# Layer 1's attention with unnormalised probabilities, divided once per eight units

## The chip, the core and the metric

The kernel runs on one NeuronCore of a Trainium2 chip. The metric is the time of one execution in microseconds of the device; the median of three runs of the kernel before is 2408.08 us (2406.07 to 2408.76). The core has five engines with queues of their own, which run in order and wait for each other by semaphores: TensorE (PE; its weight loads are listed as PEld), VectorE (DVE), ScalarE (ACT), GpSimd (POOL) and SyncE (SP), which here issues the transfers. Matmul results land in PSUM, everything else lives in SBUF.

## The reference

A two-layer encoder over 1024 positions of width 1024. Layer 1 mixes with windowed attention (16 query heads in 4 groups that share keys and values, window +-128, a learned sink logit per head), layer 2 with dilated attention; each layer ends in a SwiGLU network. What the change touches is the attention of layer 1, cut to its core:

```
s = einsum('nbqhgd,nbkhd->nbhgqk', qb, kw) * (dh ** -0.5) + bias      # 128 queries x 384 keys
m = max(s.max(axis=-1), sink)
p = exp(s - m)
l = p.sum(axis=-1) + exp(sink - m)
o = einsum('nbhgqk,nbkhd->nbqhgd', p, vw) / l
```

All of it is float32. The kernel keeps that accuracy on PE by splitting each operand into a rounded high part and a low remainder, and by multiplying the parts.

## The kernel before

Layer 1's attention is `layer_a`. Its work comes in 32 units: 2 halves of the sequence (t), 4 key heads (hd), 4 blocks of 128 queries each (b). A unit has two parts, written as generators that yield between steps. `first` calls `probs`: for each of the 4 query heads g, two matmuls write the scores 128 queries x 384 keys (256 at the sequence's ends) into a PSUM tile ps_s (two buffers); DVE adds the bias, takes the negated maximum and writes the tile p (line 509); ACT takes the exponential and the sum l (line 519). Then the kernel before forms the denominator: n plus the sink (line 516), its exponential (517), the sum (522), the reciprocal (523), and it scales the four tiles p, three on DVE (526) and one on ACT (528).

`second` calls `weigh` two units later: for each block of 128 keys PE transposes the four tiles p into ps_t (548, two buffers), ACT copies the high part to pp (550), DVE subtracts for the low part (551), and two matmuls weigh the values into ps_o (542). The values hold high and low parts side by side, so ps_o has the two halves of a sum in its two halves of partitions; ACT copies one (563), DVE adds the other (564) into os. ACT and POOL split os into the two parts of oT (813, 814), which the output projection reads.

Between these steps `weave` places fill work by the table FILL_A: the projections of the second half's queries, the output projection of the first half (`out_0`, whose result is added to x by line 370 and squared for the norm of the next network), and the first matmuls of that network. A scheduler orders the instructions of each engine from this text with costs of its own, and gives tiles their buffers: p has a ring of 11, the bias tiles one of 6, and the general tiles t2 (os, the rows of x and their squares) one of 4.

After the last unit the queue is emptied: the norm of the first half (rms on PE and POOL, `modulate` on DVE and ACT), the first matmuls of the network (`up_early`), the last weighings, and the output projection of the second half. Its weights pass through ACT (179) and POOL (180), which split them as well.

Of the kernel before, what the change touches and what calls it, by code (L numbers as in the profile page):

```python
# [74 lines left out]
class Trunk:  # L75
# [419 lines left out]
    def probs(self, psp, att, qs, kh, kl, lo, hi, bias, sink, n, l, width, bufs, zero=None):  # L495


        nc = self.nc
        per, np = bufs
        tiles = [att.tile([P, per, width], F, name="p", tag="p", bufs=np) for _ in range(4 // per)]  # L500
        pt = [p[:, g] for p in tiles for g in range(per)]
        for p in tiles if zero else ():
            nc.gpsimd.memset(p[:, :, zero], 0.0)
        for g in range(4):
            ps = psp.tile([P, HT], F, name="ps_s", tag="s", bufs=2)
            nc.tensor.matmul(ps[:, lo:hi], lhsT=qs[g], rhs=kh, start=True, stop=False)  # L506
            mm = nc.tensor.matmul(ps[:, lo:hi], lhsT=qs[g], rhs=kl, start=False, stop=True)
            self.marks.append(mm.ins)
            nc.vector.tensor_tensor_reduce(pt[g][:, lo:hi], ps[:, lo:hi], bias[g][:, lo:hi], -1.0,  # L509
                                           -NEG if sink is None else sink[1][:, g:g + 1],  # L510
                                           op0=ALU.add, op1=ALU.min, accum_out=n[:, g:g + 1])
            yield
        if sink is not None:
            st = att.tile([P, 2, 4], F, name="st", tag="st", bufs=6)
            e, r = st[:, 0], st[:, 1]
            nc.vector.tensor_tensor(e, sink[0], n, op=ALU.add)
            nc.scalar.activation(e, e, AF.Exp)
        for g in range(4):
            nc.scalar.activation(pt[g][:, lo:hi], pt[g][:, lo:hi], AF.Exp, bias=n[:, g:g + 1], scale=-1.0, accum_out=l[:, g:g + 1])
        if sink is None:  # L520
            return pt
        nc.vector.tensor_tensor(l, l, e, op=ALU.add)
        nc.vector.reciprocal(r, l)
        for g in range(4):
            if g < 3:
                nc.vector.tensor_scalar(pt[g][:, lo:hi], pt[g][:, lo:hi], r[:, g:g + 1], None, op0=ALU.mult)  # L526
            else:
                nc.scalar.activation(pt[g][:, lo:hi], pt[g][:, lo:hi], AF.Copy, scale=r[:, g:g + 1])
        return pt

    def weigh(self, psp, att, pt, chunks, out, low, par):
# [191 lines left out]
    def layer_a(self, h, x_src):  # L723
# [65 lines left out]
        self.norm_bank = self.bank  # L789
        wp, wk = (es.enter_context(sb(n)) for n in ("probs_a", "work_a"))  # L790
        self.raw = deque([(self.main, 1)])
        dist = wp.tile([P, 384], F, name="dist")
        nc.sync.dma_start(dist, a["dist"][:, 0:384])

        def first(hd, b, bias):
# [1 line left out]
            lo, hi = (0 if b > 0 else P), (384 if b < 7 else 256)  # L797
            k0 = (b - 1) * P
            c = slice((b % 4) * P, (b % 4) * P + P)
            ml = wp.tile([P, 2, 4], F, name="ml", tag="ml", bufs=6)  # L800
            return self.probs(psp, wp, [q[(p, g, par, t)][:, c] for g in range(4)], kh[hd][:, k0 + lo:k0 + hi], kl[hd][:, k0 + lo:k0 + hi],
                              lo, hi, bias, [self.sink[:, s, 4 * hd:4 * hd + 4] for s in range(2)], ml[:, 0], ml[:, 1], 384, (1, 11))

        def second(hd, b, pt, oT):
            p, par = hd // 2, hd % 2
            own, other = head_rows(par)
            cs = [c for c in range(3) if 0 <= b - 1 + c <= 7]
            os = wk.tile([P, HT], F, name="os", tag="t2", bufs=self.t2)
            osv = os.rearrange("p (g q) -> p g q", q=P)
            yield from self.weigh(psp, wk, pt, [(c * P, vt[:, b - 1 + c, hd], P) for c in cs], osv[own], osv[other], par)  # L810
            osv = osv[own]
            c = slice((b % 4) * P, (b % 4) * P + P)
            nc.scalar.activation(oT[p][0][own, :, c], osv, AF.Copy)
            nc.gpsimd.tensor_tensor(oT[p][1][own, :, c], osv, f32(oT[p][0][own, :, c]), op=ALU.subtract)

        def out_proj(ps, d, oT):
            return self.project_steps(ps, self.weight("a_w_out", d), [(oT[k // 4][0][:, k % 4], oT[k // 4][1][:, k % 4]) for k in range(KT)])
# [10 lines left out]
            if d == KT - 1:  # L828
                spill["h"] = self.norm_half(spill["x"], spill["ssq"], layer, 1, wk)

        oTs = []
        self.fill_start([q_tile(p, g, 1) for p in range(2) for g in range(4)] + [out_0(d) for d in range(KT)] + [self.up_early(layer, spill)], FILL_A, LOOK_A, 64)
        units = [(t, hd, b) for t in range(2) for hd in range(4) for b in range(4 * t, 4 * t + 4)]
        pend = deque()
        for i, (t, hd, b) in enumerate(units):
# [4 lines left out]
            if i in (16, 24):  # L840
                self.fill_until(32 * (i // 8 - 1))
            if b % 4 == 0:
                bias = self.bias_tiles(wp, dist, SLOPE_A[4 * hd:4 * hd + 4], 6, nc.vector if i < BIAS_DVE else None)
            pt = self.weave(i, first(hd, b, bias), second(*pend.popleft()) if len(pend) > 1 else None)
            pend.append((hd, b, pt, oTs[t]))
        while self.fill:
            self.fill_step()
        while pend:
            run(second(*pend.popleft()))
        es.close()  # L850
        self.kqv.close()

# [449 lines left out]
def _arrays(np, i):  # L1302
# [8 lines left out]
    def per_part(v):  # L1311
# [3 lines left out]
    o["x"] = c(i["x"][0].T).reshape(KT, P, T)  # L1315
    o["vec"] = c(np.concatenate([per_part(i["norm_mix"]), per_part(i["norm_ffn"]), per_part(i["final_norm"]),
                                 per_part(i["c"]), per_part(i["ada_b"])], axis=1))
    o["sink"] = c(i["a_sink"])
    o["cst"], o["dist"] = _constants(np)
    o["ada_w"] = c(i["ada_w"])  # L1320
# [42 lines left out]
```

## Time and profile before

| | us |
|---|---|
| median of three runs | 2408.08 |
| the profiled execution | 2409.9 |
| its span | 2408.1 |
| PE busy | 2264.6 (94%) |
| DVE busy | 1286.4 (53%) |
| ACT busy | 870.2 (36%) |
| POOL busy | 740.7 (31%) |

Times of rows are microseconds from the span's start. A row of a group gives the line of the kernel, the engine and operation, what it writes and reads, the shapes and the count; behind the first bar the busy time and the mean duration of one in ns, behind the second the idle time of that engine just before such an instruction, and who ended it. PE overlaps matmuls, so a duration can be longer than the distance to the next one.

### The profile page before, as it was taken

The numbers are of one execution on the slowest core, as the hardware profiler recorded it, in microseconds if no ns is written. First come the engines' busy times: TensorE is split into PE (matmuls) and PEld (weight loads), VectorE is DVE, ScalarE is ACT, GpSimd is POOL, SyncE is SP. The second block draws the span as 40 slices with busy tenths as digits, with TensorE's granted clock in tenths as the row PEclk, the third lists the DMA queues.
The fourth block names the chain that finished last, engine by engine and source line by source line (L and its number), as shares of the span: only waits on it lengthen the run. The fifth ranks groups of instructions, "written<-read, shape, count | busy, mean of one in ns | idle before, by whom it ended". The sixth has DMA issues, their size and how long they took to land.

```text
span 2408.1 us, 28177 instructions
## 1 busy us (share of the span) xinstructions
PE 2264.6 (94%) x10572; PEld 1874.8 (78%) x10572; DVE 1286.4 (53%) x2263; ACT 870.2 (36%) x1721; POOL 740.7 (31%) x467
## 2 busy tenths in 40 slices
PE   8699898988999999999989999787999999999997
PEld 7587676766788888888879878665788888888886
DVE  6869999688533333333362577785633332222325
ACT  2549887332111111111252788673411111111111
POOL 2525453453122122222233344344531212221210
PEclk9899999999999999999999999898999999999999
DMA  7431124666411111111234765736321111111101
GB/s 282 154 139 36 40 84 132 215 218 207 158 59 39 50 44 53 44 53 44 79 123 156 197 185 179 214 88 195 102 71 53 48 49 53 53 52 46 53 18 70
DMA packets 131225, 248.85 MB, mean 103 GB/s; under 512 B 39312, under 2 KB 66576, under 8 KB 130064
## 3 DMA queue, kind: packets, MB, share of 16 engines
q1 hardware_dynamic: 131088, 247.05, 32.1%
q8 instruction: 83, 1.36, 0.2%
q14 instruction: 54, 0.44, 0.1%
HBM read 214.20 MB, written 30.70 MB: 102 GB/s over the span
## 4 chain that ended last, share of the span: by engine, by line
PE 70%; DVE 15%; DMA 6%; issue 2%; ACT 2%; SPq 1%; POOL 0%; DVEq 0%; ACTq 0%; POOLq 0%
PE ps_d L300 22%; PE ps_d L302 22%; PE ps_d L301 22%; DMA ada_w<-in_ada_w 3%; DVE ada_acc L152 2%; DVE p L509 2%; DVE pp L551 2%; DVE p L526 1%; PE ps_o L542 1%; PE ps_t L548 1%; DVE os L564 1%; DVE ht L272 1%; DMA ml_all<-sd 1%; DVE h L278 1%; DMA al<-ad 1%
## 5 line engine op out<-in xcount | busy, mean ns | idle before, releaser
L300 PE MATMUL ps_d<-h,w 128*128 128x512 f32 x1968 | 778.1, 397 | 29.3 <-ACT w L179 14.2
L301 PE MATMUL ps_d<-h,w 128*128 128x512 f32 x1968 | 777.0, 395 | 10.9 <-DVE h L278 9.3
L302 PE MATMUL ps_d<-h,w 128*128 128x512 f32 x1968 | 773.7, 394 | 2.6 <-POOL w L180 2.6
L180 POOL TENSOR_TENSOR w<-raw,w 128x1024 fp32r<-128x1024 f32 (+1 forms) x178 | 431.7, 2427 | 786.6 <-ACT w L179 774.7
L300 PEld LDWEIGHTS ps_d<-h,w 128*128 128x128 f32 x1968 | 373.9, 190 | 101.5 <-ACT w L179 15.7
L301 PEld LDWEIGHTS ps_d<-h,w 128*128 128x128 f32 x1968 | 375.3, 191 | 83.4 <-DVE h L278 11.7
L302 PEld LDWEIGHTS ps_d<-h,w 128*128 128x128 f32 x1968 | 373.9, 190 | 82.1 <-POOL w L180 3.8
L417 DVE TENSOR_TENSOR u<-silu,ps_d 128x512 f32<-128x512 f32 x88 | 60.4, 686 | 605.9 <-PE ps_d L302 589.7
L370 DVE SCALAR_TENSOR_TENSOR x<-ps_d,mod,x 128x512 f32<-128x512 f32 x368 | 270.4, 748 | 152.0 <-PE ps_d L302 149.5
L179 ACT ACTIVATE w<-raw 128x1024 fp32r<-128x1024 f32 (+1 forms) x178 | 185.7, 1047 | 368.4 <-PE ps_d L302 295.0
L300 PE MATMUL ps_d<-act,wo 128*128 128x512 f32 x704 | 276.1, 392 | 10.0 <-DVE x L370 6.9
L302 PE MATMUL ps_d<-act,wo 128*128 128x512 f32 x704 | 275.0, 391 | 0.0
L301 PE MATMUL ps_d<-act,wo 128*128 128x512 f32 x704 | 274.9, 391 | 0.0
L180 POOL TENSOR_TENSOR wo<-raw,wo 128x1024 fp32r<-128x1024 f32 x44 | 106.4, 2417 | 432.7 <-ACT wo L179 425.2
L179 ACT ACTIVATE wo<-raw 128x1024 fp32r<-128x1024 f32 x44 | 46.7, 1061 | 382.5 <-PE ps_d L302 340.3
L300 PEld LDWEIGHTS ps_d<-act,wo 128*128 128x128 f32 x704 | 132.6, 188 | 39.5 <-DVE x L370 8.3
L302 PEld LDWEIGHTS ps_d<-act,wo 128*128 128x128 f32 x704 | 132.7, 188 | 27.7
L301 PEld LDWEIGHTS ps_d<-act,wo 128*128 128x128 f32 x704 | 132.7, 188 | 27.1
L419 DVE TENSOR_TENSOR act<-u,act 128x512 fp32r<-128x512 f32 x88 | 125.1, 1421 | 47.5 <-ACT act L418 47.4
L152 DVE SCALAR_TENSOR_TENSOR ada_acc<-ada_w,cond,ada_acc 128x1024 f32<-128x1024 f32 x70 | 125.9, 1799 | 43.2 <-DMA ada_w<-in_ada_w 42.6
L418 ACT ACTIVATE act<-u 128x512 fp32r<-128x512 f32 x88 | 55.0, 625 | 217.1 <-DVE u L417 217.1
L506 PE MATMUL ps_s<-kh,q 128*128 128x384 f32 (+3 forms) x320 | 103.6, 328 | 21.4 <-DVE stat L509 11.5
(174 smaller groups left out, 2660.1 us busy)
## 6 DMA issues: line engine op xcount, KB each, us to landing
raw<-in_ffn_w_in SPq DMA_DIRECT2D x102, 512.0 KB
ada_w<-in_ada_w SPq DMA_DIRECT2D x80, 512.0 KB
raw<-in_ffn_w_out SPq DMA_DIRECT2D x44, 512.0 KB
raw<-in_b_w_q SPq DMA_DIRECT2D x24, 512.0 KB
qd<-qo SPq DMA_DIRECT2D x48, 256.0 KB
h<-in_ada_w SPq DMA_DIRECT2D x8, 1024.0 KB
raw<-in_a_w_out SPq DMA_DIRECT2D x16, 512.0 KB
q<-qd SPq DMA_DIRECT2D x16, 512.0 KB
```

Source lines behind the costliest of these rows:

```text
L152: nc.vector.scalar_tensor_tensor(acc, w, s, acc, op0=ALU.mult, op1=ALU.add)
L179: self.nc.scalar.activation(w[:, 0], raw, AF.Copy)
L180: self.nc.gpsimd.tensor_tensor(w[:, 1], raw, f32(w[:, 0]), op=ALU.subtract)
L300: mm(ps, lhsT=w[0], rhs=x[0], start=first, stop=False)
L301: mm(ps, lhsT=w[0], rhs=x[1], start=False, stop=False)
L302: mm(ps, lhsT=w[1], rhs=x[0], start=False, stop=last)
L370: self.nc.vector.scalar_tensor_tensor(x, ps, self.mod[:, layer, c * 8 + d:c * 8 + d + 1], x, op0=ALU.mult, op1=ALU.add)
L417: nc.vector.tensor_tensor(u, s, up, op=ALU.mult)
L418: nc.scalar.activation(act[:, 0, halves(t)], u, AF.Copy)
L419: nc.vector.tensor_tensor(act[:, 1, halves(t)], u, f32(act[:, 0, halves(t)]), op=ALU.subtract)
L506: nc.tensor.matmul(ps[:, lo:hi], lhsT=qs[g], rhs=kh, start=True, stop=False)
L509: nc.vector.tensor_tensor_reduce(pt[g][:, lo:hi], ps[:, lo:hi], bias[g][:, lo:hi], -1.0, -NEG if sink is None else sink[1][:, g:g + 1], op ...
```

## The change

The probabilities of layer 1 are weighed as they come from the exponential. n and l of eight units (a pair of heads, one half of the sequence) are kept in a tile ml, the weighed sums of the eight units in a tile ou of 128 x 4 x 512 (one buffer). A new function `normalise` runs once for each such block, after unit 9, 17 and 25 and at the end: it forms the 32 denominators' reciprocals of each query in one go, splits them into high and low parts, transposes them (four 128 x 16 transposes), and multiplies the 16 rows with a matrix sel of zeros and ones, so that PE writes each reciprocal to the 64 partitions of its head. DVE multiplies ou with that, and ACT and POOL split the product. The ring of p becomes 9, that of the bias tiles 5.

```diff
@@ probs @@
             nc.vector.tensor_tensor_reduce(pt[g][:, lo:hi], ps[:, lo:hi], bias[g][:, lo:hi], -1.0,
-                                           -NEG if sink is None else sink[1][:, g:g + 1],
+                                           -NEG if sink is None else sink[:, g:g + 1],
                                            op0=ALU.add, op1=ALU.min, accum_out=n[:, g:g + 1])
             yield
-        if sink is not None:
-            st = att.tile([P, 2, 4], F, name="st", tag="st", bufs=6)
-            e, r = st[:, 0], st[:, 1]
-            nc.vector.tensor_tensor(e, sink[0], n, op=ALU.add)
-            nc.scalar.activation(e, e, AF.Exp)
         for g in range(4):
             nc.scalar.activation(pt[g][:, lo:hi], pt[g][:, lo:hi], AF.Exp, bias=n[:, g:g + 1], scale=-1.0, accum_out=l[:, g:g + 1])
-        if sink is None:
-            return pt
-        nc.vector.tensor_tensor(l, l, e, op=ALU.add)
-        nc.vector.reciprocal(r, l)
-        for g in range(4):
-            if g < 3:
-                nc.vector.tensor_scalar(pt[g][:, lo:hi], pt[g][:, lo:hi], r[:, g:g + 1], None, op0=ALU.mult)
-            else:
-                nc.scalar.activation(pt[g][:, lo:hi], pt[g][:, lo:hi], AF.Copy, scale=r[:, g:g + 1])
         return pt
@@ layer_a @@
+        sel = wp.tile([16, HT], R, name="sel")
+        raw = wk.tile([P, HT], F, name="sel_f", tag="t2", bufs=self.t2)[0:16]
+        nc.sync.dma_start(raw, a["sel"])
+        nc.scalar.activation(sel, raw, AF.Copy)
...
-            ml = wp.tile([P, 2, 4], F, name="ml", tag="ml", bufs=6)
+            if hd % 2 == 0 and b % 4 == 0:
+                mls[p, t] = wp.tile([P, 2, 2, 4, 4], F, name="ml", tag="ml", bufs=2)
+            ml = mls[p, t][:, :, par, b % 4]
...
-                              lo, hi, bias, [self.sink[:, s, 4 * hd:4 * hd + 4] for s in range(2)], ml[:, 0], ml[:, 1], 384, (1, 11))
+                              lo, hi, bias, self.sink[:, 1, 4 * hd:4 * hd + 4], ml[:, 0], ml[:, 1], 384, (1, 9))
...
-            os = wk.tile([P, HT], F, name="os", tag="t2", bufs=self.t2)
-            osv = os.rearrange("p (g q) -> p g q", q=P)
-            yield from self.weigh(psp, wk, pt, [(c * P, vt[:, b - 1 + c, hd], P) for c in cs], osv[own], osv[other], par)
-            osv = osv[own]
+            if par == 0 and b % 4 == 0:
+                outs[p, t] = wk.tile([P, 4, HT], F, name="ou", tag="ou", bufs=1)
+            low = wk.tile([P, HT], F, name="os", tag="t2", bufs=self.t2)
             c = slice((b % 4) * P, (b % 4) * P + P)
-            nc.scalar.activation(oT[p][0][own, :, c], osv, AF.Copy)
-            nc.gpsimd.tensor_tensor(oT[p][1][own, :, c], osv, f32(oT[p][0][own, :, c]), op=ALU.subtract)
+            yield from self.weigh(psp, wk, pt, [(c * P, vt[:, b - 1 + c, hd], P) for c in cs], outs[p, t][own, :, c],
+                                  low.rearrange("p (g q) -> p g q", q=P)[other], par)
+
+        def normalise(p, t, oT):
+
+            n, l = (mls[p, t][:, s] for s in range(2))
+            e = wp.tile([P, 2, 4, 4], F, name="e", tag="e", bufs=1)
+            sink = self.sink[:, 0, 8 * p:8 * p + 8].rearrange("p (h x g) -> p h x g", h=2, x=1).broadcast_to([P, 2, 4, 4])
+            nc.vector.tensor_tensor(e, sink, n, op=ALU.add)
+            nc.scalar.activation(e, e, AF.Exp)
+            nc.vector.tensor_tensor(l, l, e, op=ALU.add)
+            nc.vector.reciprocal(e, l)
+            fl = wp.tile([P, 4, 2, 8], R, name="fl", tag="fl", bufs=1)
+            ev = e.rearrange("p h b g -> p b h g")
+            hi, lo = (fl[:, :, s].rearrange("p b (h g) -> p b h g", h=2) for s in range(2))
+            nc.scalar.activation(hi, ev, AF.Copy)
+            nc.vector.tensor_tensor(lo, ev, f32(hi), op=ALU.subtract)
+            tp = psp.tile([P, HT], F, name="ps_t", tag="t", bufs=2)
+            for b in range(4):
+                nc.tensor.transpose(tp[0:16, b * P:(b + 1) * P], f32(fl[:, b]).rearrange("p s x -> p (s x)"), self.ident)
+            rows = wk.tile([P, HT], R, name="rows", tag="t2", bufs=self.t2)[0:16]
+            nc.scalar.activation(rows, tp[0:16], AF.Copy)
+            for g in range(4):
+                ps = psp.tile([P, HT], F, name="ps_r", tag="s", bufs=2)
+                nc.tensor.matmul(ps, lhsT=sel[:, g * P:(g + 1) * P], rhs=rows, start=True, stop=True)
+                o = wk.tile([P, HT], F, name="os", tag="t2", bufs=self.t2)
+                nc.vector.tensor_tensor(o, outs[p, t][:, g], ps, op=ALU.mult)
+                nc.scalar.activation(oT[p][0][:, g], o, AF.Copy)
+                nc.gpsimd.tensor_tensor(oT[p][1][:, g], o, f32(oT[p][0][:, g]), op=ALU.subtract)
...
-                bias = self.bias_tiles(wp, dist, SLOPE_A[4 * hd:4 * hd + 4], 6, nc.vector if i < BIAS_DVE else None)
+                bias = self.bias_tiles(wp, dist, SLOPE_A[4 * hd:4 * hd + 4], 5, nc.vector if i < BIAS_DVE else None)
             pt = self.weave(i, first(hd, b, bias), second(*pend.popleft()) if len(pend) > 1 else None)
-            pend.append((hd, b, pt, oTs[t]))
+            pend.append((hd, b, pt))
+            if i % 8 == 1 and i > 1:
+                normalise(i // 8 % 2 ^ 1, (i - 2) // 16, oTs[(i - 2) // 16])
...
             run(second(*pend.popleft()))
+        normalise(1, 1, oTs[1])
```

In the rows of the order that follow, the new kernel's lines are numbered anew: its 514 is the exponential (before 519), 528 the weighing (542), 534 the transpose (548), 537 the low part pp (551), 550 the sum of the two halves, now into ou (564), 828 the spread matmul into ps_r, 830 the product.

DVE near the end of the units, before, up to the last addition to x (line 370), where ISA is the score read:

```order
L526 TENSOR_SCALAR p<-p,st 128x384 x3
L509 ISA p,ml<-ps_s,bias,sink 128x256
L509 ISA ml 128x1
L509 ISA p,ml<-ps_s,bias,sink 128x256
L509 ISA ml 128x1
L551 TENSOR_TENSOR pp<-ps_t,pp 128x512
L564 TENSOR_TENSOR os<-ps_o,os 64x512
L370 SCALAR_TENSOR_TENSOR xst<-ps_d,mod,xst 128x512
```

The same place now, from the first score read of the last unit on:

```order
L509 ISA p,ml<-ps_s,bias,sink 128x256
L509 ISA ml 128x1
L550 TENSOR_TENSOR ou<-ps_o,os 64x4x128
L537 TENSOR_TENSOR pp<-ps_t,pp 128x512
L370 SCALAR_TENSOR_TENSOR xst<-ps_d,mod,xst 128x512
L509 ISA p,ml<-ps_s,bias,sink 128x256
L509 ISA ml 128x1
```

The three scalings are gone, and the addition stands ahead of the last unit's second score read.

PE among the scores of units 8 to 11 before: scores (506, 507), fill (300 to 302), weighing and transposes:

```order
L507 MATMUL ps_s<-kl_85,q 128x384
L300 MATMUL ps_d<-h,w 128x512
L301 MATMUL ps_d<-h,w 128x512
L302 MATMUL ps_d<-h,w 128x512
L548 MATMUL ps_t<-cst,p 128x128 x4
L542 MATMUL ps_o<-pp,vt 128x512 x3
L548 MATMUL ps_t<-cst,p 128x128 x4
L506 MATMUL ps_s<-kh_81,q 128x384
```

PE at the first block now, which stands among the scores of the same units:

```order
L302 MATMUL ps_d<-h,w 128x512
L528 MATMUL ps_o<-pp,vt 128x512 x2
L534 MATMUL ps_t<-cst,p 128x128 x4
L828 MATMUL ps_r<-rows,sel 128x512 x2
L534 MATMUL ps_t<-cst,p 128x128 x4
L528 MATMUL ps_o<-pp,vt 128x512 x2
L534 MATMUL ps_t<-cst,p 128x128 x4
L528 MATMUL ps_o<-pp,vt 128x512
L828 MATMUL ps_r<-rows,sel 128x512 x2
L528 MATMUL ps_o<-pp,vt 128x512 x2
L534 MATMUL ps_t<-cst,p 128x128 x4
L506 MATMUL ps_s<-kh_81,q 128x384
```

The spread matmuls come in two pairs, and no score or fill matmul stands from the first pair until the row after the second.

PE between the first matmuls of the network and the output projection, before:

```order
L301 MATMUL ps_d<-h,w 128x512
L302 MATMUL ps_d<-h,w 128x512
L542 MATMUL ps_o<-pp,vt 128x512 x4
L300 MATMUL ps_d<-h,w 128x512
L301 MATMUL ps_d<-h,w 128x512
```

And now:

```order
L302 MATMUL ps_d<-h,w 128x512
L528 MATMUL ps_o<-pp,vt 128x512 x4
L828 MATMUL ps_r<-rows,sel 128x512 x4
L300 MATMUL ps_d<-h,w 128x512
L301 MATMUL ps_d<-h,w 128x512
```

The four spread matmuls of the last block stand between the last weighing and the output projection.

## Rows read from the trace of the kernel before

**Rows 1.** The page's first line.

```profile
span 2408.1 us, 28177 instructions
```

**Rows 2.** Stretches: PE, PEld, DVE, ACT, POOL busy (instructions), PE clock, DMA, GB/s.

```profile
165.00:394.50 229.50, 212.94 (x1110) 172.79 (x1111) 221.35 (x564) 199.39 (x480) 104.64 (x71) 0.99 0.19 61
394.50:416.20 21.70, 14.21 (x71) 10.56 (x69) 18.58 (x41) 14.27 (x31) 6.30 (x15) 0.84 0.58 195
...
660.00:720.00 60.00, 60.00 (x267) 49.69 (x266) 23.03 (x26) 10.86 (x14) 14.93 (x7) 1.00 0.19 59
1332.00:1500.00 168.00, 164.17 (x926) 137.33 (x925) 115.84 (x380) 140.39 (x393) 68.70 (x58) 0.99 0.66 188
```

**Rows 3.** Groups on DVE, 165 to 394.5 us.

```profile
L551 DVE TENSOR_TENSOR pp<-ps_t,pp 128x512 fp32r<-128x512 f32 x79 | 54.0, 684 | 0.8 <-ACT pp L550 0.2
L526 DVE TENSOR_SCALAR p<-p,st 128x384 f32<-128x384 f32 x69 | 37.8, 603 | 0.4
...
L516 DVE TENSOR_TENSOR st<-sink,ml 128x4 f32<-128x4 f32 x30 | 12.9, 431 | 0.1
...
L522 DVE TENSOR_TENSOR ml<-ml,st 128x4 f32<-128x4 f32 x30 | 9.3, 310 | 0.1
L526 DVE TENSOR_SCALAR p<-p,st 128x256 f32<-128x256 f32 x21 | 7.6, 420 | 0.2
L523 DVE RECIPROCAL st<-ml 128x4 f32<-128x4 f32 x30 | 5.3, 176 | 0.7
```

**Rows 4.** Groups on PE, 165 to 394.5 us.

```profile
L542 PE MATMUL ps_o<-pp,vt 128*128 128x512 f32 x158 | 62.6, 430 | 9.4 <-DVE pp L551 8.9 <-ACT pp L550 0.3
...
L506 PE MATMUL ps_s<-kh,q 128*128 128x384 f32 x96 | 36.5, 380 | 3.4 <-DVE ml L509 3.1
...
L506 PE MATMUL ps_s<-kh,q 128*128 128x256 f32 x27 | 8.8, 328 | 3.0 <-DVE ml L509 3.0
```

**Rows 5.** Groups on ACT, then on POOL, 165 to 394.5 us.

```profile
L550 ACT ACTIVATE pp<-ps_t 128x512 fp32r<-128x512 f32 x80 | 46.7, 587 | 3.3 <-PE ps_t L548 2.5
...
L813 ACT ACTIVATE h<-os 64x512 fp32r<-64x512 f32 x28 | 17.6, 627 | 6.1 <-DVE os L564 5.6
...
L528 ACT ACTIVATE p<-p,st 128x384 f32<-128x384 f32 x23 | 13.9, 606 | 0.1
...
L814 POOL TENSOR_TENSOR h<-os,h 64x512 fp32r<-64x512 f32 x28 | 36.1, 1288 | 75.4 <-ACT h L813 71.2 <-DMA raw<-in_a_w_out 3.7
```

**Rows 6.** Timeline of DVE, then of POOL: start, us, instruction.

```profile
326.52 1.08 DVE L526 TENSOR_SCALAR p<-p,st 128x384 f32<-128x384 f32 x3
...
396.95 3.17 DVE L526 TENSOR_SCALAR p<-p,st 128x384 f32<-128x384 f32 x3
...
397.55 2.36 POOL L180 TENSOR_TENSOR w<-raw,w 128x1024 fp32r<-128x1024 f32 x1 [4.01 <-ACT w L179]
```

**Rows 7.** Timeline at the stage's end: PE, SP and DVE.

```profile
394.25 0.39 PE L302 MATMUL ps_d<-h,w 128*128 128x512 f32 x1
...
395.44 0.42 SPq L585 DMA_DIRECT2D xst<-in_x  x1
...
402.28 0.75 DVE L370 SCALAR_TENSOR_TENSOR xst<-ps_d,mod,xst 128x512 f32<-128x512 f32 x1
...
406.56 0.95 PE L222 MATMUL ps_d<-ones,ssq 128*128 128x1 f32 x8
...
411.58 1.16 PE L260 MATMUL ps_d<-cst,st 128*128 128x128 f32 x8 [0.93 <-POOL st L257]
...
416.22 0.57 PE L301 MATMUL ps_d<-h,w 128*128 128x512 f32 x1 [1.38 <-DVE h L278]
```

**Rows 8.** Timeline at the output projection of the second half.

```profile
428.97 1.09 PE L542 MATMUL ps_o<-pp,vt 128*128 128x512 f32 x4
...
430.82 0.68 DVE L564 TENSOR_TENSOR os<-ps_o,os 64x512 f32<-64x512 f32 x1 [0.89 <-ACT os L563]
...
431.56 0.50 PE L300 MATMUL ps_d<-h,w 128*128 128x512 f32 x1 [1.50 <-DVE os L564]
...
434.43 2.37 POOL L180 TENSOR_TENSOR w<-raw,w 128x1024 fp32r<-128x1024 f32 x1
```

More of the change, by code (lines that the diff above doesn't have):

```diff
@@ L804, in second @@
-        def second(hd, b, pt, oT):
-            p, par = hd // 2, hd % 2
+                              lo, hi, bias, self.sink[:, 1, 4 * hd:4 * hd + 4], ml[:, 0], ml[:, 1], 384, (1, 9))
+        def second(hd, b, pt):
+            p, par, t = hd // 2, hd % 2, b // 4
             own, other = head_rows(par)
             cs = [c for c in range(3) if 0 <= b - 1 + c <= 7]
-            os = wk.tile([P, HT], F, name="os", tag="t2", bufs=self.t2)
-            osv = os.rearrange("p (g q) -> p g q", q=P)
-            yield from self.weigh(psp, wk, pt, [(c * P, vt[:, b - 1 + c, hd], P) for c in cs], osv[own], osv[other], par)
-            osv = osv[own]
+            if par == 0 and b % 4 == 0:
+                outs[p, t] = wk.tile([P, 4, HT], F, name="ou", tag="ou", bufs=1)
+            low = wk.tile([P, HT], F, name="os", tag="t2", bufs=self.t2)
@@ L829, in out_0 @@
                 spill["h"] = self.norm_half(spill["x"], spill["ssq"], layer, 1, wk)
-        oTs = []
+        oTs, mls, outs = [], {}, {}
         self.fill_start([q_tile(p, g, 1) for p in range(2) for g in range(4)] + [out_0(d) for d in range(KT)] + [self.up_early(layer, spill)], FILL_A, LOOK_A, 64)
@@ L1317, in _arrays @@
                                  per_part(i["c"]), per_part(i["ada_b"])], axis=1))
+    o["sel"] = np.kron(np.ones((2, 1)), np.kron(np.eye(8).reshape(8, 2, 4).transpose(0, 2, 1).reshape(8, 8), np.ones((1, 64)))).astype(np.float32)
     o["sink"] = c(i["a_sink"])
```

## The prediction

> **What bounds the kernel now.** I read the page's span line first, then the busy times by stage, then the groups of DVE, PE, ACT and POOL inside the stage that the change touches, and last the timeline around the stage's end. The span is 2408.1 us [rows 1], the profiled execution took 2409.9, the median of three runs is 2408.08; so the execution on which I work lies 1.8 us above the median, and I take that off at the end.
>
> The change touches layer 1's attention: 32 units, woven with projection matmuls, from about 160 us until the last weighing near 430 us. From 165 to 394.5 us DVE is busy 221.35 of 229.5 us (96%), PE 212.94 (93%), ACT 199.39 (87%) [rows 2]. The kernel is bound by PE elsewhere: from 660 to 720 us it never stops, 267 matmuls in 60.00 us, 0.225 us each [rows 2]. Here PE has 16.56 us of idle time, and what ends it is DVE: the weighing matmuls waited 8.9 us for DVE's pp, the score matmuls 3.1 and 3.0 us for its score reads [rows 4]. So a saving on DVE is worth, in this stretch, at most what PE still loses; the rest of it turns into DVE idle time.
>
> A second place follows. PE's last fill matmul of this stage starts at 394.25, but DVE adds that result to x only at 402.28. Its input was loaded by an SP transfer issued at 395.44, and DVE was in between with three scalings that took 3.17 us together [rows 6, 7]. From that addition hangs a serial chain: sum of squares on PE at 406.56, its broadcast at 411.58, the next projection at 416.22 [rows 7]. In 394.5 to 416.2 PE is busy only 14.21 of 21.7 us, at a granted clock of 0.84 [rows 2].
>
> **What the change removes on DVE.** Up to 394.5 us: the scalings 37.8 + 7.6, the sink addition 12.9, the denominator 9.3, the reciprocal 5.3: 72.9 us [rows 3]. Much of that is waiting inside the instruction: three 128x384 scalings took 1.08 us at 326.52 and 3.17 us at 396.95, where a GpSimd subtraction of 2.36 us began at 397.55 [rows 6].
>
> **What it adds on DVE.** Per block of eight units, four products 128x512 with one operand in PSUM, like the pp subtraction, 0.684 each, and four operations on 128x32. The trace has no 128x32; its 128x4 ones average 0.176 to 0.431 [rows 3], which bounds the four by 0.7 and 1.7 us. A block is 3.4 to 4.4 us; I take 4. Three of the four blocks stand inside the stretch: 12 us. DVE falls from 221 to about 160 us of work and is no longer the bound.
>
> **ACT and POOL.** ACT loses in the stretch the fourth scaling (13.9 us and the 128x256 ones) and the copies of os (17.6), and gains per block one 16x512 and four 128x512 copies near 0.6 [rows 5]: some 20 us less. POOL loses 36.1 us and gains 12 subtractions of 128x512; the row of 64x512 has 1.288 us [rows 5], bounds 1.2 to 2.4 (half of, and the whole of, the 128x1024 one at 2.36 [rows 6]): 14 to 29 us. Both have room; hidden behind PE. The selector's load and copy at the stage's start are one transfer and one 16x512 copy: 0 to 2 us, taken as 0, hidden by DVE's work before the first softmax.
>
> **What it adds on PE.** Per block four transposes and four 128x512 matmuls: at most 8 x 0.225 = 1.8 us; three blocks 5.4 us.
>
> **Term 1, the stretch to 394.5.** PE then has 212.9 + 5.4 = 218.3 us of work. What idle share remains? The nearest row is the next layer's attention, 1332 to 1500 us, same weaving, no scaling of probabilities: DVE 69%, ACT 84%, PE 164.17 of 168 us, so 2.3% idle [rows 2]. With that share 218.3 / 0.977 = 223.4 us, 6.1 less than 229.5. The blocks bring a new wait: in PE's order the third and fourth spread matmul share two PSUM buffers with the first two, so they stand behind two products on DVE, and weighing, transposes and scores queue behind them. The path is the copy of rows (0.6), a pp copy before the product (0.587), its subtraction (0.684) and two products (1.37): 3.2 us, against PE's own work in between, two spread and three weighing matmuls and eight transposes: 1.1 us for the five 512-wide ones alone, 2.9 if a transpose took as long; 1.9 taken. So 1.3 us a block, half of it inside the 2.3% already counted: 2 us for three blocks. Against that, the granted clock is 0.99 over the 229.5 us [rows 2], which is 1.1 to 3.4 us lost to stretches at 1.2 of 2.4 GHz; with fewer pauses I let 1.7 go. Sum: -6.1 + 2 - 1.7, about **-6**. Bounds: all idle time gone, -11; nothing gained and each block waiting 4 us, +8 with the blocks' own work hidden in the idle time.
>
> The Trainium skill ("Perfetto Trace Analysis", section "Identifying the Most-Contended Engine") says that matmul busy time is a poor measure of TensorE's headroom and that the share of LDWEIGHTS is a better one. By that measure the stretch stands at 172.79 of 229.5 us, 75%, and the next layer's attention at 137.33 of 168, 82% [rows 2]; reaching the same share would give -13 instead of -6. The mixes differ (weights of a transpose load in less time), so I keep the matmul rows.
>
> **Term 2, the chain at the end.** In DVE's order the last addition to x stands before behind three scalings, two score reads, a pp and an os; after, behind one score read, an ou and a pp. It waited from 394.64 to 402.28, 7.6 us. The SP transfer limits the gain: it is queued behind the store and reload of the row block before, whose own addition was late by the same backlog. I take **-6**, bounds -2 (the transfer still decides) and -8. The 5.0 us of GpSimd arithmetic and the 4.6 us to the next projection stay.
>
> **Term 3, the last block.** The fourth block has nothing to hide behind. Before, the last weighing starts at 428.97, os ends at 431.50, and the output projection begins at 431.56 [rows 8]. After, two of the four spread matmuls wait for two products, 2 x 0.69, on the same path: +1.6 us. Behind it POOL has four subtractions in place of one, so the weights of the next projection, begun at 434.43 [rows 8], come 4 to 5 us later against some 2.6 us of slack. Together 2 to 5 us; against it, less of this is seen if the modulation transfers that follow set the pace. I take **+2**, bounds -1 and +5.
>
> Sum -6 - 6 + 2 = -10: 2409.9 - 10 = 2399.9 for this execution, 2398 against the median.
>
> **Rivals.** A difference under 0.2%, 4.8 us, can't be told from none.
> - *PE is freed altogether.* For it: almost every PE wait above names DVE, and the LDWEIGHTS share. Against: ACT stays at 80%, and pp needs ACT and then DVE whatever DVE's load. The far bounds, -11 - 8 - 1 = -20: 2388.
> - *The hop stays.* The wait before weighing is for pp, made by ACT (0.587) and then DVE (0.684), and neither is changed. If these 8.9 us stay and the last block costs 4: -2 - 4 + 4 = -2: 2406. Against it: DVE's subtraction started late because of the queue in front of it.
> - *Slower: the shorter ring of probability tiles.* Nine tiles instead of eleven at four a unit: only the first score read of a unit finds a free tile; the other three need the last transposes of the unit two before. If that makes one read per unit late by its own length (0.61 + 0.08), 29 units cost 20 us: 2398 + 20 = 2418. It decides from (10 + 4.8) / 29 = 0.5 us per unit. For it: PE now stands in order behind those transposes, and the bias ring is shorter too. Against: the transposes no longer wait for scalings, so they come earlier.
>
> **Chances.** Forecast 0.63 (own range 2391 to 2403), freed 0.14, hop stays 0.14, slower 0.09. Faster by more than 0.2%: 0.77; within: 0.14; slower: 0.09. Leaving a tenth out on each side: 2387 to 2408.
>
> **What would show it.** DVE busy near 160 us in the stretch and PE idle near 5; the waits of weighing for pp down to a third. The last addition to x within 2 us of the last fill matmul, and PE's clock there still below full. A gap before the output projection about 1.6 us longer. Wrong if score matmuls wait for score reads more than now (the ring), if PE waits over 2 us at each set of spread matmuls, or if the stages from 480 us on don't simply move earlier.

## The result

The changed kernel takes 2388.53 us, the median of four runs (2386.59 to 2388.72), against 2408.42 for the kernel before (four runs, 2406.07 to 2409.90): ratio 0.9918, 95% interval 0.9906 to 0.9930, so 19.9 us faster. Forecast were 2398 us, range 2387 to 2408. The direction and the three places hold, and the time lies in the range, near its lower end; it lies outside the forecast's own range of 2391 to 2403. The gain is about twice the forecast, and 2388 was the price of the rival "PE is freed altogether".

The profiled execution took 2388.49 us, 21.4 less than the one of before. The page of the changed kernel begins so [rows 1]:

```profile
span 2386.7 us, 28047 instructions
```

The same stretches as in [rows 2], moved to where their work now stands (the stage up to its last fill matmul; the serial chain; the projections up to the output projection; the next layer's attention). Columns as in [rows 2]:

```profile
165.00:378.40 213.40, 208.55 (x1127) 174.83 (x1126) 168.75 (x409) 177.17 (x420) 82.87 (x53) 0.99 0.21 67
378.40:392.90 14.50, 10.25 (x64) 7.63 (x63) 11.79 (x25) 9.73 (x22) 4.96 (x14) 0.96 0.68 247
392.90:410.90 18.00, 16.03 (x55) 12.10 (x55) 10.87 (x17) 7.17 (x12) 2.59 (x2) 0.85 0.05 10
1310.00:1478.00 168.00, 163.38 (x916) 136.54 (x915) 113.15 (x371) 138.07 (x386) 67.77 (x57) 0.98 0.67 187
```

DVE is busy 168.75 of 213.40 us, 79% instead of 96%. PE has 4.85 us idle, the 2.3% of the forecast, though 3.8 of it are the new wait for the rows of reciprocals (L828 below). But its busy time fell from 212.94 to 208.55 although the change gave it more matmuls: the busy time of before held waiting. The share of LDWEIGHTS went from 75 to 82%, to that of the next layer.

Groups on PE, 165 to 378.4 us, against [rows 4]:

```profile
L528 PE MATMUL ps_o<-pp,vt 128*128 128x512 f32 x161 | 62.8, 425 | 0.0
L534 PE MATMUL ps_t<-cst,p 128*128 128x128 f32 x324 | 50.5, 275 | 0.5 <-ACT p L514 0.5
...
L506 PE MATMUL ps_s<-kh,q 128*128 128x384 f32 x95 | 34.9, 368 | 0.5 <-DVE ml L509 0.4
...
L506 PE MATMUL ps_s<-kh,q 128*128 128x256 f32 x25 | 7.5, 302 | 0.0
...
L828 PE MATMUL ps_r<-rows,sel 16*128 16x512 f32 x12 | 4.8, 478 | 3.8 <-ACT rows L825 3.8
```

The 8.9 us for pp are gone, the 6.1 us of the score matmuls are down to 0.4. On DVE, against [rows 3]:

```profile
L537 DVE TENSOR_TENSOR pp<-ps_t,pp 128x512 fp32r<-128x512 f32 x81 | 55.8, 688 | 5.7 <-ACT pp L536 4.9
...
L830 DVE TENSOR_TENSOR os<-ou,ps_r 128x512 f32<-128x512 f32 x12 | 7.7, 682 | 1.6 <-PE ps_r L828 1.5
...
L815 DVE RECIPROCAL e<-ml 128x32 f32<-128x32 f32 x3 | 1.1, 353 | 0.1
L812 DVE TENSOR_TENSOR e<-sink,ml 128x32 f32<-128x32 f32 x3 | 1.0, 349 | 0.0
```

DVE now stands idle where it was queued up. Timeline at the end of the stage, against [rows 7] (start, us, instruction):

```profile
373.90 0.42 SPq L571 DMA_DIRECT2D xst<-in_x  x1
...
378.70 0.40 PE L302 MATMUL ps_d<-h,w 128*128 128x512 f32 x1
...
379.43 0.74 DVE L370 SCALAR_TENSOR_TENSOR xst<-ps_d,mod,xst 128x512 f32<-128x512 f32 x1
...
383.31 0.94 PE L222 MATMUL ps_d<-ones,ssq 128*128 128x1 f32 x7 [0.51 <-DVE ssq L218]
...
388.28 0.93 PE L260 MATMUL ps_d<-cst,st 128*128 128x128 f32 x6 [0.21 <-POOL st L257]
...
392.91 0.80 PE L301 MATMUL ps_d<-h,w 128*128 128x512 f32 x1 [1.38 <-DVE h L278]
```

The last fill matmul starts 15.6 us earlier (394.25 to 378.70), the last addition 22.9 (402.28 to 379.43): its distance from the matmul fell from 8.0 to 0.7 us. And at the output projection, against [rows 8]:

```profile
406.31 1.09 PE L528 MATMUL ps_o<-pp,vt 128*128 128x512 f32 x4
...
408.06 0.59 ACT L825 ACTIVATE rows<-ps_t 16x512 fp32r<-16x512 f32 x1
...
408.70 0.73 PE L828 MATMUL ps_r<-rows,sel 16*128 16x512 f32 x2 [1.29 <-ACT rows L825]
...
409.97 1.09 PE L828 MATMUL ps_r<-rows,sel 16*128 16x512 f32 x2 [0.55 <-DVE os L830]
...
410.99 0.50 PE L300 MATMUL ps_d<-h,w 128*128 128x512 f32 x1
```

From the last weighing to the output projection it is 4.68 us, before 2.59. What follows moves along: the output projection is 20.6 us earlier, the end of the span 21.4.

### The profile page after: what moved, and what is told of

It reads as the page before. It is cut to its first block, busy times and chain, and to the rows that moved or that the text cites. A ratio compares the mean times of both kernels' runs of the same rounds, so it can differ in the third digit from the quotient of the medians.

```text
span 2386.7 us, 28047 instructions
## 1 busy us (share of the span) xinstructions
PE 2265.4 (95%) x10604; PEld 1878.6 (79%) x10604; DVE 1229.5 (52%) x2103; ACT 845.4 (35%) x1654; POOL 719.9 (30%) x451
## 4 chain that ended last, share of the span: by engine, by line
PE 75%; DVE 9%; DMA 6%; issue 2%; ACT 2%; POOL 1%; SPq 0%; DVEq 0%; ACTq 0%; POOLq 0%
PE ps_d L300 23%; PE ps_d L302 23%; PE ps_d L301 23%; DMA ada_w<-in_ada_w 3%; DVE ada_acc L152 2%; PE ps_o L528 2%; PE ps_t L534 2%; PE ps_s L507 1%; PE ps_s L506 1%; DMA ml_all<-sd 1%; DVE ht L272 1%; DVE p L509 1%; DVE h L278 1%; DVE pp L537 1%; DVE x L370 1%
## 5 line engine op out<-in xcount | busy, mean ns | idle before, releaser
L302 PE MATMUL ps_d<-h,w 128*128 128x512 f32 x1968 | 774.8, 394 | 2.8 <-POOL w L180 2.7
L302 PEld LDWEIGHTS ps_d<-h,w 128*128 128x128 f32 x1968 | 374.5, 190 | 83.8 <-POOL w L180 4.9
L302 PE MATMUL ps_d<-act,wo 128*128 128x512 f32 x704 | 274.6, 390 | 0.0
L302 PEld LDWEIGHTS ps_d<-act,wo 128*128 128x128 f32 x704 | 132.6, 188 | 27.8
L537 DVE TENSOR_TENSOR pp<-ps_t,pp 128x512 fp32r<-128x512 f32 x168 | 115.3, 688 | 15.6 <-ACT pp L536 13.7
```

Of the source, the lines that this page charges most:

```text
L302: mm(ps, lhsT=w[1], rhs=x[0], start=False, stop=last)
L537: nc.vector.tensor_tensor(pp[n, 1], tp[n], f32(pp[n, 0]), op=ALU.subtract)
```

## The experiments

The stage is measured from DVE's first score read (L509) to the start of PE's last fill matmul (L302). That keeps two things out: the first score read came anywhere from 157.18 to 162.35 us in these profiles, and layer 2 has a wait of its own (below). The stage is from one profile each; the ratio to the kernel before is from all runs, each group with its own runs of the kernel before beside it (medians 2409.03 for e1 to e4, 2410.70 for e6 to e8, 2409.12 for e9 to e11, 2412.39 for e12), so ratios can be compared and medians less well.

Two things limit what a stage of one profile can tell. The runs of one variant lie up to 13 us apart (e8: 2388.46 to 2401.79), and the profiled one can be the slowest (e4, e7's first, e8, e12). And each variant is a program in which the scheduler laid the instructions out anew: counted from the traces by tile and shape, at least 202 of PE's 1140 instructions of the stage stand elsewhere in e3's order, 200 in e9's, 134 in e2's, 100 in e1's, 60 in e12's, 35 in e7's first, and none in e4's. A difference of a few us can come from that.

| kernel | stage, us | DVE busy in it | PE clock | median, us | ratio (95%) |
|---|---|---|---|---|---|
| before | 233.89 | 223.28 | 0.99 | 2408.42 | 1 |
| changed | 220.77 | 173.32 | 0.99 | 2388.53 | 0.9918 (0.9906-0.9930) |
| e1, three scalings back | 236.21 | 216.02 | 0.98 | 2402.45 | 0.9967 (0.9957-0.9978) |
| e2, before without them | 217.82 | 184.62 | 1.00 | 2392.27 | 0.9932 (0.9920-0.9945) |
| e3, before, small rings | 251.62 | 227.38 | 0.97 | 2426.62 | 1.0071 (1.0058-1.0083) |
| e4, before, five work tiles | 235.77 | 224.02 | 0.98 | 2416.43 | 1.0021 (1.0010-1.0032) |
| e6, rows early | 220.69 | 174.20 | 1.00 | 2388.52 | 0.9916 (0.9897-0.9936) |
| e7, one scaling back | 230.32 | 195.28 | 0.99 | 2392.76 | 0.9930 (0.9908-0.9951) |
| e7, two back | 236.39 | 207.98 | 0.97 | 2409.53 | 0.9996 (0.9983-1.0009) |
| e8, eight tiles | 227.26 | 177.31 | 0.97 | 2395.94 | 0.9943 (0.9922-0.9963) |
| e9, e2 with small rings | 222.20 | 184.06 | 1.00 | 2398.22 | 0.9955 (0.9939-0.9971) |
| e10, load off the path, six | 257.41 | 247.38 | 0.97 | 2417.35 | 1.0040 (1.0026-1.0053) |
| e11, ten tiles, four biases | 223.77 | 176.30 | 0.98 | 2392.39 | 0.9928 (0.9914-0.9942) |
| e12, load off the path, three | 239.37 | 208.44 | 0.99 | 2401.09 | 0.9949 (0.9929-0.9968) |

**e1: the scalings' load put back into the changed kernel.**

```
 # probs, after the four exponents
+for g in range(3 if sink is not None else 0):
+    nc.vector.tensor_scalar(pt[g][:, lo:hi], pt[g][:, lo:hi], self.ones[:, 0:1], None, op0=ALU.mult)
```

> The changed kernel with DVE's three scalings per unit put back, by 1.0, so that only their load and their place before the transposes return: 96 instructions, which took 0.36 to 0.6 us each on 128x384 before, 35 to 47 us of DVE in the stage. Theory A (DVE set the pace of the stage, and PE's busy time of before held waits for it): DVE stands at 168.75 + 45 = 214 us again in a stretch of 213, so it sets the pace; the stage's last fill matmul comes 8 to 12 us later, the last addition to x waits again some 3 us, 2398 to 2404 us in all, DVE over 95% busy. Theory B (the gain comes from the other removals: the small chain of sink, denominator and reciprocal, ACT's and POOL's lighter load): at most 4 us slower than the changed kernel, 2389 to 2393, with PE over 96% busy as in the changed kernel.

The stage takes 15.4 us longer than in the changed kernel, 2.3 more than in the kernel before: all of the gain is gone, though ACT (182.36 us) and GpSimd (87.79) keep their lighter load. Theory B falls. Theory A has the direction, not every size: the last fill matmul comes 17.1 us later, not 8 to 12, and DVE is 91% busy, not over 95%. By the ratios e1 is only 12 us slower than the changed kernel. Its output projection starts 21.5 us later (432.44 against 410.99), and 7.5 us of that are made up behind it, in layer 2, where SP's transfers stand in another order in this program. PE's longest wait for a weight there is 8.96 us in the changed kernel and 11.73 in the kernel before; in e1 that wait is 1.98, with another of 2.63 ahead of it. In e1 the row reads:

```profile
1651.61 0.50 PE L300 MATMUL ps_d<-h,w 128*128 128x512 f32 x1 [1.98 <-ACT w L179]
```

and in the changed kernel:

```profile
1636.86 0.80 PE L300 MATMUL ps_d<-h,w 128*128 128x512 f32 x1 [8.96 <-ACT w L179]
```

So a variant's total can be off by some 7 us through what happens far behind the stage, and the stage is the better measure of the edit.

**e2: the scalings alone taken out of the kernel before.**

```
 for g in range(4):
-    if g < 3:
-        nc.vector.tensor_scalar(pt[g][:, lo:hi], pt[g][:, lo:hi], r[:, g:g + 1], None, op0=ALU.mult)
-    else:
+    if g == 3:
         nc.scalar.activation(...)
```

> The kernel before without DVE's three scalings per unit (three of the four heads of each layer 1 unit are left unnormalised; the fourth scaling, on ACT, and all of the small chain stay). Theory A: DVE falls from 221 to about 176 us of work in the stretch and PE sets the pace; 2390 to 2396 us, most of the 20 us of the whole change, DVE near 80% busy, and the last addition to x close behind its matmul. Theory B: the small chain and ACT hold the time; 2402 us or more.

The stage falls by 16.1 us, with ACT still at 201.41 us of work and the small chain in place. DVE's scalings account for the gain, from either side, and the ratio (0.9932) says the same as the stage. But the last addition stays late, 6.2 us after its matmul. Timeline of e2:

```profile
377.21 0.39 PE L302 MATMUL ps_d<-h,w 128*128 128x512 f32 x1
...
378.85 2.35 POOL L180 TENSOR_TENSOR w<-raw,w 128x1024 fp32r<-128x1024 f32 x1 [1.31 <-issue]
...
378.95 2.27 DVE L516 TENSOR_TENSOR st<-sink,ml 128x4 f32<-128x4 f32 x1
...
383.41 0.74 DVE L370 SCALAR_TENSOR_TENSOR xst<-ps_d,mod,xst 128x512 f32<-128x512 f32 x1
```

A sink addition on 128x4, 0.15 us where nothing disturbs it, took 2.27 beside a GpSimd subtraction. So the small chain has its share in the second term.

**e3: the changed kernel's rings in the kernel before.** Probability tiles 11 to 9, bias tiles 6 to 5.

> The kernel before with the changed kernel's rings: nine probability tiles instead of eleven, five bias tiles instead of six, nothing else. If the rings cost nothing beside a busy DVE: 2408, within 2 us. The rival of the slower side, at 0.5 us or more per unit: 2423 or more. Between them: the rings cost a part of what the rest of the change gained.

The stage is 17.7 us longer, 0.55 us per unit, and the ratio agrees: smaller rings can cost what the slower rival put on them. But not by the wait that it named. The score matmuls wait for score reads 3.1 us, as in the kernel before; it is PE's transposes that waited 0.7 us in the kernel before and now wait 9.6. First the row of before, then two of e3:

```profile
L548 PE MATMUL ps_t<-cst,p 128*128 128x128 f32 x320 | 48.9, 275 | 0.7 <-DVE p L526 0.7
...
L548 PE MATMUL ps_t<-cst,p 128*128 128x128 f32 x320 | 51.4, 282 | 9.6 <-DVE pp L551 6.4 <-DVE p L526 3.2
L506 PE MATMUL ps_s<-kh,q 128*128 128x384 f32 x96 | 36.4, 380 | 3.4 <-DVE ml L509 3.1
```

Which of the two rings does it, and how much of it is the other order of PE's instructions, no run separates. The granted clock in the stage is also lower, 0.97 against 0.99.

**e4: one more work tile in the kernel before.** `self.t2, self.sq = 5, ("t2", 5)` instead of 4.

> The kernel before with five instead of four buffers in the ring that holds os, xst, the squares and other 128x512 tiles of the stage. The prediction's second term puts the late last addition to x down to DVE's backlog, not to a late buffer: then at most 2 us are gained, 2406 to 2409. If the transfer of x waits for a buffer that a late GpSimd subtraction frees, the addition comes up to 6 us earlier: 2402 to 2404.

The last addition comes 8.0 us after its matmul, as before: no buffer holds it. Why the runs take 0.2% longer, where 2406 to 2409 was expected, stays open; in the profile 2 us of it lie ahead of the stage and 2 in it, with a granted clock of 0.98 there against 0.99.

**e6: the rows of denominators one unit earlier.** `normalise` cut in two.

```
+if i % 8 == 0 and i > 0:
+    reciprocals(i // 8 % 2 ^ 1, (i - 2) // 16)
 if i % 8 == 1 and i > 1:
-    normalise(i // 8 % 2 ^ 1, (i - 2) // 16, oTs[(i - 2) // 16])
+    spread(i // 8 % 2 ^ 1, (i - 2) // 16, oTs[(i - 2) // 16])
+reciprocals(1, 1, "s")
 ...
-normalise(1, 1, oTs[1])
+spread(1, 1, oTs[1], "stst")
```

> The changed kernel with each block's reciprocals, transposes and copy of rows made one unit earlier (for the last block ahead of the last two weighings), and the last block's spread matmuls in four PSUM buffers instead of two, so that none waits for a product. In the changed kernel PE waits 1.26, 1.25 and 1.76 us for rows ahead of the first three blocks' spread matmuls, and 1.29 + 0.55 us in the last. If these waits are lost time: 4 to 6 us gained, 2383 to 2385, with the last fill matmul of the stage near 374.5 and the first output projection some 2 us closer to the last weighing. If the stage gives the time back elsewhere (PE's order is full, other waits follow): 2387 to 2389.

In the changed kernel PE waits once a block, ahead of the first pair (the expectation has these waits 0.17 us longer than the rows):

```profile
220.05 0.73 PE L828 MATMUL ps_r<-rows,sel 16*128 16x512 f32 x2 [1.09 <-ACT rows L825]
...
275.59 0.74 PE L828 MATMUL ps_r<-rows,sel 16*128 16x512 f32 x2 [1.09 <-ACT rows L825]
...
336.03 0.73 PE L828 MATMUL ps_r<-rows,sel 16*128 16x512 f32 x2 [1.59 <-ACT rows L825]
```

In e6 they don't wait any more, the last block's four run on end, and its tail is 2.5 us instead of 4.7:

```profile
408.34 1.09 PE L528 MATMUL ps_o<-pp,vt 128*128 128x512 f32 x4
409.36 1.20 PE L831 MATMUL ps_r<-rows,sel 16*128 16x512 f32 x4
410.83 0.50 PE L300 MATMUL ps_d<-h,w 128*128 128x512 f32 x1 [0.28 <-DVE ou L550]
```

Yet the stage is the same within 0.1 us and the ratio that of the changed kernel. In the stage the weighing matmuls now wait 1.7 us (0.0 in the changed kernel); the tail's 2 us aren't seen in the median. Not shown to be a better version.

**e7: one and two scalings back.** As e1, with `range(1 ...)` and `range(2 ...)`.

> The changed kernel with one scaling by 1.0 per unit on DVE (a third of the load that cost 14 us when three were put back): DVE at about 168.75 + 15 = 184 us of a stretch of 213. Theory A (DVE costs nothing until it nears the stretch's length): the last fill matmul at 378.7, at most 1.5 us later, 2387 to 2390. Rival (every instruction put on the path of a unit costs its part, whatever the share): a third of the 17 us by which that matmul came later, 5 to 6 us, 2392 to 2394.

> The changed kernel with two scalings by 1.0 per unit on DVE: about 199 us of DVE in a stretch of 213. Theory A: at the edge, the last fill matmul 1 to 5 us later, 2389 to 2393. Rival (each costs its part): two thirds of 17 us, 11 us, 2398.

The stage grows by 9.6 and 15.6 us (three: 15.4), and the last fill matmul comes 10.2 and 14.9 us later. So theory A falls in the form in which it was put: DVE costs time well before it is full. The first scaling brings 22.0 us of DVE and costs 9.6, at 85% busy. The rival's equal steps don't fit either; the first costs most and the third nothing. Part of the second step is the clock, 0.97 in that stage against 0.99 with one scaling and 0.98 with three. By the ratios the first scaling costs 3 us and the second 16 more, so the single steps are less sure than their sum.

**e8: eight tiles in the changed kernel.** `(1, 9)` to `(1, 8)`.

> The changed kernel with eight instead of nine probability tiles. In the kernel before, two tiles and one bias tile fewer cost 17 us. If the ring still sets when score reads start in the changed kernel, one more tile taken away costs 8 us or more: 2396 or later, with score matmuls waiting for score reads. If tiles now come free early enough (no scaling between exponent and transposes): at most 3 us, 2388 to 2391.

6.5 us more, and the score matmuls don't wait for score reads (0.4 us). By its size that is between the two cases, but most of it is time at a lower clock. In e8 TensorE ran at the lower of its two clock levels, 1.2 GHz, in two stretches of the stage, PE busy throughout, each just behind a wait of 1.3 us for a block's rows:

```profile
224.00:230.80 6.80, 6.80 (x22) 4.92 (x21) 4.30 (x8) 4.56 (x8) 3.90 (x4) 0.50 0.00 0
343.40:350.20 6.80, 6.80 (x20) 4.94 (x20) 4.49 (x9) 4.32 (x8) 4.19 (x4) 0.50 0.14 39
```

In the changed kernel there is one such stretch, half as long:

```profile
337.00:340.40 3.40, 3.40 (x13) 2.26 (x10) 1.97 (x4) 2.23 (x4) 1.57 (x2) 0.50 0.31 77
```

At half the clock a busy PE loses half of such a stretch (fill matmuls start 0.43 us apart there and 0.23 just behind it): 6.8 us in e8 and 1.7 in the changed kernel. That is 5.1 of the 6.5 us, and leaves 1.4 for the missing tile, too little for one profile to show. The profiled run is the slowest of e8's six; the fastest, 2388.46 us, is no slower than the changed kernel. By the ratio eight tiles cost 6 us; whether they bring on these pauses is not shown.

**e9: e2 with nine and five tiles.** e2's edit, with e3's numbers.

> The kernel before without DVE's three scalings per unit (three of four heads of each layer 1 unit left unnormalised, as in e2), and with the changed kernel's rings: nine probability tiles, five bias tiles. From the first score read to the last fill matmul the stage took 217.8 us in e2 and 233.9 in the kernel before; in the kernel before the smaller rings cost 17.7 us of that. If the rings cost only because a tile waits for its scaling: 216 to 220 us. If the changed kernel still pays for its rings: 222 us or more.

4.4 us more than e2, a quarter of the 17.7, and just inside the second case. But the profile does not bear out a cost: e9's first score read came 2.1 us earlier than e2's and its last addition stands 2.6 us closer behind the last fill matmul, and the output projection starts at the same time. First e2, then e9:

```profile
413.05 0.50 PE L300 MATMUL ps_d<-h,w 128*128 128x512 f32 x1 [1.50 <-DVE os L562]
...
413.04 0.50 PE L300 MATMUL ps_d<-h,w 128*128 128x512 f32 x1 [1.50 <-DVE os L562]
```

The spans of the two profiles differ by 3.9 us, all of it behind that point (the ratios by 5.5). So without the scalings the smaller rings cost between nothing and 4.4 us of layer 1, and which, stays open.

**e10 and e12: the same load, off the path.** e12 with `range(3 ...)`.

```
+for _ in range(6 if sink is not None else 0):
+    nc.vector.tensor_scalar(self.vec, self.vec, self.ones[:, 0:1], None, op0=ALU.mult)
```

> The changed kernel with DVE work put back that no other engine waits for: six scalings by 1.0 of a 128x144 table per unit, in place, 192 in all, some 40 to 60 us of DVE. With three scalings of the probabilities per unit put back (49 us of DVE in the stretch, between the exponent and the transposes) the stage took 236.2 instead of 220.8 us. Load theory (DVE's queue is what counts, wherever the work stands): 232 us or more for a like load. Path theory (what counts is the time that a tile of probabilities waits between its exponent and its transposes): 221 to 225 us.

> The same as e10 with three scalings of the table per unit instead of six: 96 in all, some 45 us of DVE by the 0.47 us each that they took there, close to the 49 us in the stretch of the three scalings of the probabilities (stage 236.2 us against 220.8). In e10 the load came to 91 us, so that DVE's work alone, 173 + 91, was longer than the 257 us of the stage: that run could not tell the two theories apart. Load theory: 232 us or more from the first score read to the last fill matmul. Path theory: 221 to 225 us.

e10 brought 74 us more DVE time and 36.6 more stage; it was too much to tell. e12 brought 35.1 and cost 18.6, though nothing waits for these results: the load theory holds, the path theory falls. By the ratios e12 is only 7.5 us slower than the changed kernel; as in e1, its output projection starts 21.3 us later (432.29) and 6.6 us are made up far behind it, and the profiled run is the slowest of its five. In e12 the scalings all ran between 166.8 and 297 us, and that is where the time was lost. In that stretch, first e12, then the changed kernel:

```profile
166.00:297.00 131.00, 118.12 (x603) 93.73 (x601) 126.64 (x327) 98.68 (x234) 40.98 (x27) 0.97 0.11 33
...
166.00:297.00 131.00, 127.74 (x702) 106.98 (x701) 107.72 (x263) 114.78 (x274) 53.92 (x36) 1.00 0.13 41
```

PE works on 603 matmuls there instead of 702, and DVE is 97% busy. So e12 shows that the queue alone is enough, but on a DVE that is full for half of the stage; its 87% over the whole stage is a mean. What DVE costs below that is shown by e1, e2 and e7 alone. One of the scalings, on 128x144, and its neighbours in e12's timeline:

```profile
202.28 2.50 DVE L516 TENSOR_SCALAR vec<-vec,ones 128x144 f32<-128x144 f32 x1
202.31 2.38 POOL L180 TENSOR_TENSOR w<-raw,w 128x1024 fp32r<-128x1024 f32 x1 [13.51 <-PE ps_s L507]
204.70 0.60 DVE L509 CUSTOM_DVE_ANT_0 p<-ps_s,bias,sink 128x384 f32<-128x384 f32 x1
```

It ends 0.09 us after GpSimd's subtraction, and DVE's queue stands behind it.

**e11: ten probability tiles for a bias tile.** `(1, 9)` to `(1, 10)`, five bias tiles to four.

> The changed kernel with ten instead of nine probability tiles, paid for with four instead of five bias tiles (the memory has no more room). Eight tiles cost 6.5 us of the stage. If a tenth is worth something: 215 to 219 us of stage instead of 220.8, 2383 to 2387 in all. If nine are enough, or a head's bias now waits for the tiles of the head before: 221 us or more, 2388 or later.

The second case, and not shown to be better: 223.77 us of stage, at a granted clock of 0.98 against 0.99. Nothing that was run is shown to beat the changed kernel.

## Why the prediction came out as it did

**Term 1 was mis-sized: -6 forecast, -13.1 measured** (-15.6 at the last fill matmul, of which 2.4 lie ahead of the first score read, within the scatter of that read). The step that failed is "PE then has 212.9 + 5.4 = 218.3 us of work". Busy time isn't work. Where each matmul is given the median distance from its start to the next one's, for its line and shape, the stage of before adds up to 205.8 us, with 28.0 lost between matmuls; that of the changed kernel to 212.2, with 8.6 lost. So PE had 28 us to give back and not the 16.56 that the rows show as idle: 19.4 of them went, and 6.4 of work came, which makes 13.0 of the 13.1. The added work was sized right (5.4 taken up to the third block). The 1.7 us that the forecast let go for the clock did not come: it is 0.99 in both stretches.

The Trainium skill's rule in "Perfetto Trace Analysis", section "Identifying the Most-Contended Engine", was weighed in the prediction and set aside there: LDWEIGHTS share instead of matmul busy time, which gave -13. The trace agrees with it: 174.83 of 213.40 us, 82%. The working of that -13 is not shown in the prediction: 172.79 us at 82% is a stretch of 211.4, 18 us less, and only with the blocks' 5.4 us on top does it come to -13.

The reason given, DVE's load, holds (e1, e2, e7, e12), but not as a bound that is there or gone ("no longer the bound"). In e1, e2, e7, e10 and e12 each us of DVE time put in or taken out moved the stage by 0.36 to 0.53 us on the mean (15.4 for 42.7 in e1, 18.6 for 35.1 in e12), with DVE 79 to 96% busy over the stage; the clock's share in that is not taken out. With the 0.42 of e2, the change's 50.0 us less are worth 21 us; smaller rings take up to 4 of it (e9) and the blocks' matmuls up to 6, which leaves 11 to 21: an estimate in which the 13.1 measured lie.

**Term 2 was right:** -6 forecast, 7.3 us measured between the last fill matmul and the last addition, 7.8 to the next projection. The transfer of x was issued at 373.90, well ahead. e4 excludes a late buffer; e2 shows that the small chain held the addition back too, not the scalings alone.

**Term 3 was right in its size, and partly by luck:** +2 forecast, +2.1 measured. But the matmuls wait first for the copied rows (1.29) and only then for a product (0.55), and the later weights, which the forecast counted too, cost nothing that shows: from the start of the output projection to the end of the span it is 1975.7 us now and 1976.6 before.

**The wait in each block** was put at 1.3 us, and 1.09, 1.09 and 1.59 are measured, again at another place: the first pair waits for rows, not the second pair for products. The size was luck. e6, without these waits, is no faster.

**The rivals.** "Freed altogether" came true in its size, but by another sum: its -11 was all the idle time of the rows, which -13.1 goes beyond, and its -1 for the last block was +2.1. The argument against it, ACT, didn't count: e2 kept ACT at 92% of the stage. "The hop stays" is refuted by 8.9 going to 0.0. Smaller rings cost 17.7 us in the kernel before (e3) and at most some 4 once three of the four scalings are gone (e9). That fits the argument against this rival, that transposes without scalings free tiles sooner; as the scheduler's order changed too, it is not shown to be the cause.

**The signs** that were named came as forecast: PE idle 4.85 us (about 5), DVE 169 us (near 160), the last addition 0.3 us behind the end of the last fill matmul, PE's clock behind it 0.96 and 0.85, PE's wait at each set of spread matmuls under 2 us, and later stages that move along. Only the wait for pp fell further than to a third.

The sum: -13.1 - 7.8 + 2.1 = -18.8, with the 2.4 ahead of the stage -21.2, of the 21.4 between the two profiles.

## What to carry to other kernels

A matmul engine's busy time can hold waits; compare the start-to-start distances of like matmuls, or the LDWEIGHTS share, before the headroom is priced. Work on an engine that is 80 to 95% busy beside a full TensorE isn't hidden: here each us of it moved the stage by 0.36 to 0.53 us on the mean, and work that nothing waited for cost time as well where it filled the queue. A ring of buffers is priced together with what holds its tiles: the same smaller rings cost 18 us with the scalings and at most about 4 without. And before a few us are put down to an edit, look at the granted clock of the stretch and at a later common point: most of e8's 6.5 us was clock, and e9's 4.4 were gone at the output projection.

## What the hardware showed that was not expected

Some DVE instructions that work in SBUF alone are stretched while GpSimd works. In the attention stage of before, 31 of the 96 scalings overlap in the trace with a GpSimd instruction and took 0.94 us on the mean, up to 2.55; the 65 others 0.39, up to 0.42. The sink addition on 128x4: 0.59 (19, up to 3.10) against 0.16 (13). The denominators: 0.54 (12, up to 2.27) against 0.16 (20). Together (the counts by the differences) some 30 us of the removed DVE time was waiting. The reciprocal, which has one input, is not stretched (0.175 and 0.178), nor the pp subtraction, which reads PSUM and SBUF (0.684 and 0.685).

The Trainium skill ("SBUF — State Buffer", section "SBUF: two separate sides") describes an exclusive lock on a port pair that VectorE and GpSimd share, held for a whole instruction, for VectorE's two-port modes and for two SBUF inputs. The rows agree for the additions, which have two inputs in SBUF (2.27 us beside a 2.35 us subtraction in e2), and for the pp subtraction, which has only one and goes free. The scalings have one tensor as input and are stretched (2.50 us beside 2.38 in e12); that they run in such a mode no row says.
